# Sample attention of the even mixer: four sequences side by side in four column groups, page transposes placed behind the queries

## The chip, the core and the metric

The kernel runs on one core of one Trainium2 chip. The metric is the device time of one execution in microseconds (us). Engines are named as in the profile: PE (TensorE matmuls), PEld (TensorE weight loads), DVE (VectorE), ACT (ScalarE), POOL (GpSimd), SP (SyncE, which issues most DMAs).

## What is computed

The reference is one inference step of a two-layer decoder trunk for a prompt of 512 tokens and for 8 short sample sequences of 4 tokens each. The 32 sample tokens ride beside the prompt as columns 512 to 543 of every activation. Layer 0 (even) has a stick-breaking attention beside an RG-LRU; layer 1 (odd) a gated DeltaNet. A SwiGLU block stands before and behind each mixer.

The change touches one part: the attention of the sample tokens over their cached past. Each of the 8 sequences has 256 past positions in two pages of 128, found through a page table:

```python
past_k = cache_k[e][page_table].reshape(nb_s, n_pages * PAGE_SIZE, SB_HEADS, SB_HEAD_DIM)
past_v = cache_v[e][page_table].reshape(nb_s, n_pages * PAGE_SIZE, SB_HEADS, SB_HEAD_DIM)
...
z = jnp.einsum('bqhd,bshd->bhqs', q, k, preferred_element_type=jnp.float32) * (SB_HEAD_DIM ** -0.5)
z = z + bias.astype(jnp.float32)[None, :, None, None]
mask = k_pos[None, :] < q_pos[:, None]
log_keep = jnp.where(mask, jax.nn.log_sigmoid(-z), 0.0)
later = lax.cumsum(log_keep, axis=3, reverse=True) - log_keep
w = jnp.where(mask, jnp.exp(jax.nn.log_sigmoid(z) + later), 0.0)
return jnp.einsum('bhqs,bshd->bqhd', w.astype(v.dtype), v)
```

## The kernel before

All large products are three fp32r matmuls each (high and low halves of both operands): `mm3`, lines 362 to 364, output tile `lin`, with 256 or 288 columns a pass. Almost all of the kernel's time is these. The weights come in by `W` (tile `raw`, by SP), are split by ACT (line 323, `wh`) and DVE (line 324, `wl`). The output goes to one of two PSUM buffers in the even mixer, and DVE takes it away (line 646 for queries, keys and values).

The even mixer (`even_mixer`) issues its steps in the order of a string:

```python
EVEN_ORDER = "Q0 L0 V0 A0 Q1 V1 A1 Q2 X0 L1 F L2 G0 G1 G2 L3 X1 X2 G3 X3 E S0 S1 S2 V2 S3 A2 Q3 K0 V3 P2 P3 K1 A3 W U P0 P1 O1 T O0"
```

Q, V, L and X are projections, A0 to A3 the prompt's attention for one pair of heads each (`prompt_attention`: tiles `z` and `pv`, softmax-like chains on ACT and DVE between the matmuls), S the LRU scans on DVE. K0 and K1 are the sample scores of four sequences each, W the weights from them, U the sums over the values. O1 and O0 are the two halves of the output projection: O1 takes the LRU's part, O0 the attention's, whose second column half holds the sample tokens and so needs U's result.

A list scheduler turns this into one fixed order for each engine: it takes instructions by the priority of the string as soon as its own model says that their inputs and buffers are there, and may pull later work forward. Within an engine the instructions then run in that order, and each waits for semaphores that were set when the program was built.

**Scores, `sample_scores` (lines 741 to 763).** For each sequence `b` and each of its two pages: `page` (line 736) issues an indirect DMA of 256 KB by POOL into a tile of 128 positions by 512 (8 heads of 64); four transposes on PE (line 751) put it into PSUM tile `tp`; ACT (line 755) or DVE (line 753) copies it to `kt`. Then four matmuls in plain fp32 (line 758, tile `sc`), one for each pair of heads, accumulate the sequence's 32 rows (8 heads by 4 queries) by 256 positions. The output stands in partitions 32(b mod 4) to 32(b mod 4)+31, so the matmul uses one 32-wide column group of the array. DVE copies each sequence's rows to `zs` (line 759). A plain fp32 matmul is two passes (two records in the profile); the fp32r ones are one.

**Values, `sample_values` (lines 788 to 814).** For each half of four sequences the weights are transposed into `wT`; then for each sequence and page a value page is fetched and one fp32 matmul of 512 columns (line 805, tile `po`) adds into the sequence's 32 partitions. A last matmul (line 806) adds the step's own four tokens, DVE copies `po` to `os` (line 807), and 32 small matmuls (line 812, tile `oT`) turn it round for O0; ACT and DVE split it into `yh` and `yl` (lines 370, 371).

**Page buffers.** Pages share the tag `XP` with the LRU's tiles and with `wT`. There are `PB = 6` of these buffers. A page's DMA waits until the buffer's previous tenant has been read for the last time. PSUM tiles `tp`, `sc`, `sn`, `po` and `oT` share one buffer (tag `s`); `pv` has one of its own.

Of the kernel before, what the change touches and what calls it, by code (L numbers as in the profile page):

```python
# [7 lines left out]
F32 = mybir.dt.float32  # L8
# [3 lines left out]
AF = mybir.ActivationFunctionType  # L12
# [3 lines left out]
P = 128  # L16
# [330 lines left out]
def mm3(E, ws, xh, xl, evac, ks=None, halves=(0, 1)):  # L347

    nc = E.nc
    for h in halves:  # L350
        c0, cn = HALVES[h]
        use = ks[h] if ks is not None else None
        terms = [(w, k) for w in ws for k in w.at if use is None or k in use]
        if use is not None:
            terms.sort(key=lambda t: use.index(t[1]))
        E.nlin += 1
        ps = E.lin[E.nlin % len(E.lin)].tile([P, REST], F32, tag="lin", name=E.nm("lin"))[:, :cn]
        n = ws[0].h.shape[2]
        for i, (w, k) in enumerate(terms):
            wh, wl = w.h[:, w.at[k]], w.l[:, w.at[k]]  # L360
            rh, rl = xh[k][:, c0:c0 + cn], xl[k][:, c0:c0 + cn]
            nc.tensor.matmul(ps[:n], lhsT=wh, rhs=rh, start=(i == 0), stop=False)  # L362
            nc.tensor.matmul(ps[:n], lhsT=wh, rhs=rl, start=False, stop=False)  # L363
            nc.tensor.matmul(ps[:n], lhsT=wl, rhs=rh, start=False, stop=(i == len(terms) - 1))  # L364
        evac(h, c0, cn, ps)


def split_to(E, yh, yl, src, eng="act"):
    nc = E.nc
    nc.scalar.activation(yh, src, AF.Copy)  # L370
    nc.vector.tensor_tensor(yl, src, yh.bitcast(F32), op=ALU.subtract)  # L371
# [11 lines left out]
def ffn_body(E, w_in, w_out, nxt, w0=None, pre=None, mid=None, store=False):  # L383
    nc, tc = E.nc, E.tc
    with tc.tile_pool(name=E.nm("ffn"), bufs=1) as fp:
# [8 lines left out]
        for m in range(16):  # L394
            wg, wu = w0 if m == 0 else (W(E, w_in[:, o:o + P]) for o in (m * P, DFF + m * P))
            sg = fp.tile([P, NT], F32, tag="sg", name=E.nm("sg"), bufs=2)
            pr = fp.tile([P, NT], F32, tag="pr", name=E.nm("pr"), bufs=2)

            def ev_g(h, c0, cn, ps):
                s = sg[:, c0:c0 + cn]  # L400
                nc.vector.tensor_tensor(s, ps, E.rstd[:, c0:c0 + cn], op=ALU.mult)  # L401
                E.act(s, s, AF.Silu)

            def ev_u(h, c0, cn, ps):
                p_ = pr[:, c0:c0 + cn]
                nc.vector.tensor_tensor(p_, ps, E.rstd[:, c0:c0 + cn], op=ALU.mult)  # L406
                nc.vector.tensor_tensor(p_, p_, sg[:, c0:c0 + cn], op=ALU.mult)  # L407
                split_to(E, hh[m][:, c0:c0 + cn], hl[m][:, c0:c0 + cn], p_)

            mm3(E, [wg], E.xh, E.xl, ev_g)  # L410
            mm3(E, [wu], E.xh, E.xl, ev_u)
        if mid is not None:
            mid()
        for m in range(KD):
            ws = []
            for g in range(2):
                w = W(E, w_out[g * D:(g + 1) * D, m * P:(m + 1) * P])
                w.at = {k + 8 * g: i for k, i in w.at.items()}
                ws.append(w)

            def ev(h, c0, cn, ps):
                xx = E.x[m][:, c0:c0 + cn]
                nc.vector.scalar_tensor_tensor(xx, ps, 0.5, xx, op0=ALU.mult, op1=ALU.add)  # L423

            mm3(E, ws, hh, hl, ev)
            if nxt is not None:
                split_x(E, m, *nxt)
            if store:
                store_tile(E, m, *(fp.tile([P, NT], F32, tag=t, name=E.nm("out"), bufs=2) for t in ("sg", "pr")))
# [303 lines left out]
def page(E, ap, name, o):  # L733

    t = ap.tile([P, NE], F32, tag="XP", name=E.nm("page"), bufs=PB)[:, :512]
    E.nc.gpsimd.indirect_dma_start(out=t, out_offset=None, in_=E.I[name].rearrange("a n s h d -> (a n s) (h d)"),
                                   in_offset=bass.IndirectOffsetOnAxis(ap=E.idx[:, o:o + 1], axis=0))
    return t


def sample_scores(E, ap, qb, ks, zs, hf):

    nc = E.nc
    for b in range(4 * hf, 4 * hf + 4):
        rows = slice(32 * (b % 4), 32 * (b % 4) + 32)
        kt = ap.tile([P, 4, 256], F32, tag="kt", name=E.nm("kt"))
        for i in range(2):
            kp = page(E, ap, "cache_k", 2 * b + 1 - i)
            tp = E.pm.tile([P, 4, P], F32, tag="s", name=E.nm("tp"))
            for p in range(4):  # L750
                nc.tensor.transpose(tp[:, p], kp[:, p * P:(p + 1) * P], E.ident)
            if i:
                nc.vector.tensor_copy(kt[:, :, P:], tp)
            else:
                nc.scalar.activation(kt[:, :, :P], tp, AF.Copy)
        ps = E.pm.tile([P, 256], F32, tag="s", name=E.nm("sc"))
        for p in range(4):
            nc.tensor.matmul(ps[rows], lhsT=qb[p][:, b], rhs=kt[:, p], start=(p == 0), stop=(p == 3))  # L758
        nc.vector.tensor_copy(zs[rows, hf, :256], ps[rows])
    ps = E.pm.tile([P, NS], F32, tag="s", name=E.nm("sn"))  # L760
    for p in range(4):
        nc.tensor.matmul(ps, lhsT=qb[p][:, 4 * hf:4 * hf + 4].rearrange("p a b -> p (a b)"), rhs=ks[:, p], start=(p == 0), stop=(p == 3))
    nc.vector.tensor_tensor(zs[:, hf, 256:], ps, E.newmask[:, hf], op=ALU.add)
# [23 lines left out]
def sample_values(E, ap, zs, vs, yh, yl):  # L787
    nc = E.nc
    os = ap.tile([P, 2, 512], F32, tag="kt", name=E.nm("os"))
    for hf in range(2):  # L790
        wps = E.m([P, 2, P])
        for i in range(2):
            nc.tensor.transpose(wps[:, i], zs[:, hf, P * i:P * i + P], E.ident)
        wps2 = E.m([NS, P])
        nc.tensor.transpose(wps2, zs[:, hf, 256:], E.ident)
        wT = ap.tile([P, NE], F32, tag="XP", name=E.nm("wT"), bufs=PB)[:, :3 * P].rearrange("p (a b) -> p a b", a=3)
        nc.vector.tensor_copy(wT[:, :2], wps)
        nc.gpsimd.memset(wT[NS:64, 2], 0.0)
        nc.scalar.activation(wT[:NS, 2], wps2, AF.Copy)
        po = E.pm.tile([P, 512], F32, tag="s", name=E.nm("po"))  # L800
        for g in range(4):
            b = 4 * hf + g
            for i in range(2):
                vp = page(E, ap, "cache_v", 2 * b + 1 - i)
                nc.tensor.matmul(po[32 * g:32 * g + 32], lhsT=wT[:, i, 32 * g:32 * g + 32], rhs=vp, start=(i == 0), stop=False)  # L805
        nc.tensor.matmul(po, lhsT=wT[:64, 2], rhs=vs[:64], start=False, stop=True)
        nc.vector.tensor_copy(os[:, hf], po)
    oT = E.pm.tile([P, 4, NS], F32, tag="s", name=E.nm("oT"))
    for hf in range(2):
        for h in range(8):  # L810
            j = h % 2
            nc.tensor.matmul(oT[64 * j:64 * j + 64, h // 2, 16 * hf:16 * hf + 16], lhsT=os[:, hf, 64 * h:64 * h + 64], rhs=E.sel[:, h], start=True, stop=True)
    for p in range(4):
        split_to(E, yh[p][:, T:], yl[p][:, T:], oT[:, p])
# [8 lines left out]
def even_mixer(E, w_in, w_out, nxt):  # L823
    nc, tc, O = E.nc, E.tc, E.O
    with tc.tile_pool(name=E.nm("evy"), bufs=1) as yp:
# [3 lines left out]
        with E.phase(4, 2), tc.tile_pool(name=E.nm("att"), bufs=1) as ap:  # L829
# [51 lines left out]
            for tok in EVEN_ORDER.split():  # L881
# [7 lines left out]
                elif c == "L":  # L889
                    L[i] = lru_linear(E, ap, w_in, i)  # L890
                elif c == "X":
                    X[i] = lru_gate_in(E, ap, w_in, i)
                elif c == "F":
                    gw = lru_gate_weights(E)
                    E.table("sigmoid_and_others")
                elif c == "G":
                    gate[i] = lru_gates(E, ap, gw, i, *L[i])
                elif c == "E":
                    E.table("gelu_apprx_tanh_and_others")
                    for t in range(4):  # L900
                        E.act(X[t], X[t], AF.Gelu_apprx_tanh)
                    E.table(LNEXP)
                elif c == "S":
                    lru_scan(E, i, *gate[i], X[i])
                elif c == "T":
                    lru_state(E)
                elif c == "P":
                    split_to(E, yh[4 + i], yl[4 + i], X[i])
                elif c == "K":
                    if i == 0:  # L910
                        zs = ap.tile([P, 2, 288], F32, name="zs")
                    sample_scores(E, ap, qb, ks, zs, i)
                elif c == "W":
                    sample_weights(E, ap, zs)
                elif c == "U":
                    sample_values(E, ap, zs, vs, yh, yl)
                elif c == "O":
                    out(i)
# [748 lines left out]
```

## Time and profile before

| | us |
|---|---|
| median of 3 runs | 1933.24 (1932.34 to 1935.51) |
| profiled execution | 1937.59 |
| its span (first to last instruction) | 1935.8 |
| PE busy in the span | 1878.8 (97%) |
| DVE, ACT, POOL busy | 1082.1, 836.9, 125.1 |
| mean granted share of TensorE's clock | 0.989 |

The chain of work that ended last runs through PE for 84% of the span. The places of the change lie at 320 to 326 us and at 383 us (a few page transposes that the scheduler pulled forward), at 483 to 555 us (K0 and K1) and at 563 to 596 us (U). In the timeline a row is the engine's start, length, line, operation, tiles, shape and count, with the idle time before it and what ended that in brackets. A matmul's length holds its whole pipeline; what it costs in a stream is the distance from its start to the start of the next.

### The profile page before, as it was taken

To read this page: it belongs to the slowest core of one execution; us is meant where nothing else is said; L and a number is where in the kernel's file an instruction comes from. 1 tells how busy PE (TensorE), PEld (TensorE's weight loads), DVE (VectorE), ACT (ScalarE), POOL (GpSimd) and SP (SyncE) were. 2 spreads that over 40 slices of the span, in tenths; PEclk is the share of its full clock that TensorE was granted. 3 is DMA by queue.
4 is the path that set the end of the run, shared out by engine and by line. 5 is a ranking of instruction groups with operands and counts; after the bars stand their busy time and mean duration, and the time that the engine had idled before them with its cause. 6 is when DMAs were issued, how large, how long until landed. Compare 5 with 4: busy or idle time off the path is not lost.

```text
span 1935.8 us, 36595 instructions
## 1 busy us (share of the span) xinstructions
PE 1878.8 (97%) x15037; PEld 1799.5 (93%) x15037; DVE 1082.1 (56%) x2563; ACT 836.9 (43%) x1733; POOL 125.1 (6%) x237
## 2 busy tenths in 40 slices
PE   7999999999899999999999999899998997999999
PEld 6999999889668999999999999899998997999998
DVE  7444334786756544433544433688978858444422
ACT  6333324777744433322433322466675646333221
POOL 0000002111320000000000000112111100000000
PEclk9999999999999999999999999899999998999999
DMA  4333233322332333323333322333343322233332
GB/s 131 89 87 90 77 88 94 90 59 73 88 103 84 88 88 88 88 81 89 102 88 88 88 81 78 89 86 94 97 132 78 94 78 66 80 88 88 87 111 67
DMA packets 315972, 171.03 MB, mean 88 GB/s; under 512 B 28470, under 2 KB 310278, under 8 KB 315804
## 3 DMA queue, kind: packets, MB, share of 16 engines
q1 hardware_dynamic: 313244, 160.30, 29.5%
q0 software_dynamic: 2560, 8.39, 1.5%
q8 instruction: 118, 1.93, 0.4%
q14 instruction: 50, 0.41, 0.1%
HBM read 158.01 MB, written 10.65 MB: 87 GB/s over the span
## 4 chain that ended last, share of the span: by engine, by line
PE 84%; DVE 8%; ACT 4%; DMA 2%; issue 2%; POOL 1%; SPq 0%; ACTq 0%; DVEq 0%; POOLq 0%
PE lin L362 25%; PE lin L363 24%; PE lin L364 24%; DVE wl L324 1%; PE pv L729 1%; PE sc L758 1%; PE po L805 1%; DVE LT L1224 1%; DVE acc L1106 1%; DMA raw<-in_w_in_odd 1%; DVE ltmp L1223 1%; ACT wh L323 1%; PE s L1451 1%; DMA raw<-in_w_ffn_in 0%; PE m L1183 0%
## 5 line engine op out<-in xcount | busy, mean ns | idle before, releaser
L362 PE MATMUL lin<-xh,wh 128*128 128x256 f32 (+2 forms) x2992 | 875.1, 293 | 19.1 <-DVE sz L1537 4.5
L363 PE MATMUL lin<-xl,wh 128*128 128x256 f32 (+2 forms) x2992 | 872.8, 292 | 0.6 <-DVE xl L371 0.3
L364 PE MATMUL lin<-xh,wl 128*128 128x256 f32 (+2 forms) x2992 | 867.1, 290 | 0.5 <-DVE wl L324 0.5
L362 PEld LDWEIGHTS lin<-xh,wh 128*128 128x128 f32 (+1 forms) x2992 | 566.8, 190 | 25.9 <-ACT wh L323 9.0
L364 PEld LDWEIGHTS lin<-xh,wl 128*128 128x128 f32 (+1 forms) x2992 | 567.8, 190 | 5.9 <-issue 4.1
L363 PEld LDWEIGHTS lin<-xl,wh 128*128 128x128 f32 (+1 forms) x2992 | 566.9, 189 | 4.5 <-issue 1.7
L323 ACT ACTIVATE wh<-raw 128x1024 fp32r<-128x1024 f32 x261 | 275.8, 1057 | 498.9 <-PE lin L363 419.4
L324 DVE TENSOR_TENSOR wl<-raw,wh 128x1024 fp32r<-128x1024 f32 x261 | 317.7, 1217 | 89.9 <-PE lin L364 88.0
L362 PE MATMUL lin<-hh,wh 128*128 128x288 f32 (+1 forms) x1024 | 295.7, 289 | 0.0
L363 PE MATMUL lin<-hl,wh 128*128 128x288 f32 (+1 forms) x1024 | 295.4, 288 | 0.0
L364 PE MATMUL lin<-hh,wl 128*128 128x288 f32 (+1 forms) x1024 | 294.9, 288 | 0.0
L363 PEld LDWEIGHTS lin<-hl,wh 128*128 128x128 f32 x1024 | 193.0, 188 | 0.2
L364 PEld LDWEIGHTS lin<-hh,wl 128*128 128x128 f32 x1024 | 192.7, 188 | 0.1
L362 PEld LDWEIGHTS lin<-hh,wh 128*128 128x128 f32 x1024 | 192.5, 188 | 0.1
L401 DVE TENSOR_TENSOR sg<-lin,rstd 128x256 f32<-128x256 f32 (+1 forms) x128 | 55.9, 438 | 162.5 <-PE lin L364 162.4
L406 DVE TENSOR_TENSOR pr<-lin,rstd 128x256 f32<-128x256 f32 (+1 forms) x128 | 56.5, 441 | 155.9 <-PE lin L364 155.7
L370 ACT ACTIVATE hh<-pr 128x256 fp32r<-128x256 f32 (+1 forms) x128 | 55.1, 431 | 202.4 <-DVE pr L407 202.1
L423 DVE SCALAR_TENSOR_TENSOR x<-lin,x 128x256 f32<-128x256 f32 x64 | 28.2, 441 | 168.7 <-PE lin L364 168.7
L371 DVE TENSOR_TENSOR hl<-pr,hh 128x256 fp32r<-128x256 f32 (+1 forms) x128 | 56.6, 442 | 61.9 <-ACT hh L370 61.8
L100 ACT ACTIVATE sg<-sg 128x256 f32<-128x256 f32 (+1 forms) x128 | 53.7, 422 | 54.8 <-DVE sg L401 54.8
L267 ACT ACTIVATE xh<-x,vec 128x544 fp32r<-128x544 f32 (+2 forms) x64 | 39.6, 632 | 75.1 <-DVE x L423 59.3
L1106 DVE SCALAR_TENSOR_TENSOR acc<-XP,cw,acc 128x568 f32<-128x568 f32 x72 | 58.8, 817 | 2.1 <-ACT acc L1104 1.8
(480 smaller groups left out, 2098.5 us busy)
## 6 DMA issues: line engine op xcount, KB each, us to landing
raw<-in_w_ffn_in SPq DMA_DIRECT2D x128, 512.0 KB
raw<-in_w_ffn_out SPq DMA_DIRECT2D x64, 512.0 KB
raw<-in_w_in_odd SPq DMA_DIRECT2D x32, 512.0 KB
raw<-in_w_in_even SPq DMA_DIRECT2D x20, 512.0 KB
raw<-in_w_out_even SPq DMA_DIRECT2D x8, 512.0 KB
S<-in_state_dn_S SPq DMA_DIRECT2D x8, 512.0 KB
out_dn_S_sample<-S SPq DMA_DIRECT2D x8, 512.0 KB
raw<-in_w_out_odd SPq DMA_DIRECT2D x8, 512.0 KB
```

The lines of the kernel that those rows point to most:

```text
L100: i = self.nc.scalar.activation(out, in_, func, **kw).ins
L267: nc.scalar.activation(xh, x, AF.Copy, scale=g)
L323: nc.scalar.activation(self.h, raw, AF.Copy)
L324: nc.vector.tensor_tensor(self.l, raw, self.h.bitcast(F32), op=ALU.subtract)
L362: nc.tensor.matmul(ps[:n], lhsT=wh, rhs=rh, start=(i == 0), stop=False)
L363: nc.tensor.matmul(ps[:n], lhsT=wh, rhs=rl, start=False, stop=False)
L364: nc.tensor.matmul(ps[:n], lhsT=wl, rhs=rh, start=False, stop=(i == len(terms) - 1))
L370: nc.scalar.activation(yh, src, AF.Copy)
L371: nc.vector.tensor_tensor(yl, src, yh.bitcast(F32), op=ALU.subtract)
L401: nc.vector.tensor_tensor(s, ps, E.rstd[:, c0:c0 + cn], op=ALU.mult)
L406: nc.vector.tensor_tensor(p_, ps, E.rstd[:, c0:c0 + cn], op=ALU.mult)
L1106: nc.vector.scalar_tensor_tensor(a, XP[:, j:j + XW - 3], cw[j], a, op0=ALU.mult, op1=ALU.add)
```

## The change

Scores: for each half of four sequences and each page position `i`, four pages (one a sequence) are fetched first. For each pair of heads `p`, one PSUM tile `tp` takes one transposed block of each of the four sequences, is copied to `kt`, and four matmuls of 128 columns go to the four column groups of one PSUM tile. That tile, `sc`, now has the tag of the prompt attention's `pv`, and is copied once for all four sequences. The transposes of a tile are chained in the scheduler's order (`E.after` is an ordering edge on one engine with no semaphore), beginning with the page that is fetched last, and in K0 they may not stand ahead of the last projection matmul that was issued, that of Q3. Values: for each page position four pages are fetched, and their four matmuls are chained likewise. Number, shape and columns of the value matmuls stay; the 32 score matmuls of 256 columns become 64 of 128.

```diff
--- before.py
+++ after.py
@@ -361,7 +361,7 @@
             rh, rl = xh[k][:, c0:c0 + cn], xl[k][:, c0:c0 + cn]
             nc.tensor.matmul(ps[:n], lhsT=wh, rhs=rh, start=(i == 0), stop=False)
             nc.tensor.matmul(ps[:n], lhsT=wh, rhs=rl, start=False, stop=False)
-            nc.tensor.matmul(ps[:n], lhsT=wl, rhs=rh, start=False, stop=(i == len(terms) - 1))
+            E.last_mm = nc.tensor.matmul(ps[:n], lhsT=wl, rhs=rh, start=False, stop=(i == len(terms) - 1)).ins
         evac(h, c0, cn, ps)
 
 
@@ -741,22 +741,25 @@
 def sample_scores(E, ap, qb, ks, zs, hf):
 
     nc = E.nc
-    for b in range(4 * hf, 4 * hf + 4):
-        rows = slice(32 * (b % 4), 32 * (b % 4) + 32)
-        kt = ap.tile([P, 4, 256], F32, tag="kt", name=E.nm("kt"))
-        for i in range(2):
-            kp = page(E, ap, "cache_k", 2 * b + 1 - i)
+    sc = E.pm.tile([P, 512], F32, tag="pv", name=E.nm("sc"))[:, :256]
+    for i in range(2):
+        kp = [page(E, ap, "cache_k", 2 * (4 * hf + b) + 1 - i) for b in range(4)]
+        for p in range(4):
+            if p % 2 == 0:
+                kt = ap.tile([P, 2, 4, P], F32, tag="kt", name=E.nm("kt"))
             tp = E.pm.tile([P, 4, P], F32, tag="s", name=E.nm("tp"))
-            for p in range(4):
-                nc.tensor.transpose(tp[:, p], kp[:, p * P:(p + 1) * P], E.ident)
-            if i:
-                nc.vector.tensor_copy(kt[:, :, P:], tp)
+            tr = [nc.tensor.transpose(tp[:, b], kp[b][:, p * P:(p + 1) * P], E.ident).ins for b in (3, 0, 1, 2)]
+            for j in range(1, 4):
+                E.after(tr[j], tr[j - 1])
+            if hf == 0:
+                E.after(tr[0], E.last_mm)
+            if p % 2:
+                nc.vector.tensor_copy(kt[:, 1], tp)
             else:
-                nc.scalar.activation(kt[:, :, :P], tp, AF.Copy)
-        ps = E.pm.tile([P, 256], F32, tag="s", name=E.nm("sc"))
-        for p in range(4):
-            nc.tensor.matmul(ps[rows], lhsT=qb[p][:, b], rhs=kt[:, p], start=(p == 0), stop=(p == 3))
-        nc.vector.tensor_copy(zs[rows, hf, :256], ps[rows])
+                nc.scalar.activation(kt[:, 0], tp, AF.Copy)
+            for b in range(4):
+                nc.tensor.matmul(sc[32 * b:32 * b + 32, i * P:(i + 1) * P], lhsT=qb[p][:, 4 * hf + b], rhs=kt[:, p % 2, b], start=(p == 0), stop=(p == 3), skip_group_check=True)
+    nc.vector.tensor_copy(zs[:, hf, :256], sc)
     ps = E.pm.tile([P, NS], F32, tag="s", name=E.nm("sn"))
     for p in range(4):
         nc.tensor.matmul(ps, lhsT=qb[p][:, 4 * hf:4 * hf + 4].rearrange("p a b -> p (a b)"), rhs=ks[:, p], start=(p == 0), stop=(p == 3))
@@ -798,12 +801,12 @@
         nc.gpsimd.memset(wT[NS:64, 2], 0.0)
         nc.scalar.activation(wT[:NS, 2], wps2, AF.Copy)
         po = E.pm.tile([P, 512], F32, tag="s", name=E.nm("po"))
-        for g in range(4):
-            b = 4 * hf + g
-            for i in range(2):
-                vp = page(E, ap, "cache_v", 2 * b + 1 - i)
-                nc.tensor.matmul(po[32 * g:32 * g + 32], lhsT=wT[:, i, 32 * g:32 * g + 32], rhs=vp, start=(i == 0), stop=False)
-        nc.tensor.matmul(po, lhsT=wT[:64, 2], rhs=vs[:64], start=False, stop=True)
+        for i in range(2):
+            vp = [page(E, ap, "cache_v", 2 * (4 * hf + g) + 1 - i) for g in range(4)]
+            mm = [nc.tensor.matmul(po[32 * g:32 * g + 32], lhsT=wT[:, i, 32 * g:32 * g + 32], rhs=vp[g], start=(i == 0), stop=False, skip_group_check=True).ins for g in (3, 0, 1, 2)]
+            for j in range(1, 4):
+                E.after(mm[j], mm[j - 1])
+        nc.tensor.matmul(po, lhsT=wT[:64, 2], rhs=vs[:64], start=False, stop=True, skip_group_check=True)
         nc.vector.tensor_copy(os[:, hf], po)
     oT = E.pm.tile([P, 4, NS], F32, tag="s", name=E.nm("oT"))
     for hf in range(2):
```

Behind the even mixer the order is the same on every engine. Three places in the built order, whose names are tiles with the build's numbers:

PE in K0, before: a sequence's four score matmuls (`sc`) stand together, and transposes (`tp`) of the next sequence's pages follow at some distance (`m` is another transpose).

```order
L758 MATMUL sc_5810<-kt_5793,qb_4622 32x256
L758 MATMUL sc_5810<-kt_5793,qb_5752 32x256
L364 MATMUL lin_5901<-xh_90,wl_5871 128x288
L362 MATMUL lin_5901<-xh_91,wh_5870 128x288
L363 MATMUL lin_5901<-xl_99,wh_5870 128x288
L364 MATMUL lin_5901<-xh_91,wl_5871 128x288
L362 MATMUL lin_5901<-xh_92,wh_5870 128x288
L363 MATMUL lin_5901<-xl_100,wh_5870 128x288
L364 MATMUL lin_5901<-xh_92,wl_5871 128x288
L751 MATMUL tp_5819<-ident,page_5817 128x128 x4
```

PE in K0, now: here the last set of transposes of the first half (`tp_5861`) and what comes behind it.

```order
L761 MATMUL sc_5770<-kt_5850,qb_4622 32x128 x4
L751 MATMUL tp_5861<-ident,page_5827 128x128
L751 MATMUL tp_5861<-ident,page_5821 128x128
L751 MATMUL tp_5861<-ident,page_5823 128x128
L751 MATMUL tp_5861<-ident,page_5825 128x128
L362 MATMUL lin_6507<-xh_92,wh_6503 128x256
L721 MATMUL z_6115<-sl_6127,negtri 128x384
L725 MATMUL z_6115<-sh_6084,negones 128x128
L726 MATMUL z_6115<-sl_6085,negones 128x128
L725 MATMUL z_6115<-sh_6104,negones 128x256
L761 MATMUL sc_5770<-kt_5850,qb_5752 32x128 x4
L765 MATMUL sn_5872<-ks,qb_3639 128x32
```

The score matmuls stand in 16 sets of four. The next transposes, `tp_5964` on the pages 5961, 5955, 5957 and 5959, come behind 18 more rows (three `sn`, ten `lin`, four `z` and an identity load). What stands between sets is O1's projection (`lin_6507`), which stood in U before.

PE in U, before: around the value matmuls (`po`) of the first half's last sequence.

```order
L805 MATMUL po_6265<-page_6284,wT_6261 32x512
L363 MATMUL lin_6515<-xl_98,wh_6483 128x256
L364 MATMUL lin_6515<-xh_90,wl_6484 128x256
L720 MATMUL z_6165<-sh_6176,negtri 128x256
L362 MATMUL lin_6515<-xh_91,wh_6483 128x256
L363 MATMUL lin_6515<-xl_99,wh_6483 128x256
L364 MATMUL lin_6515<-xh_91,wl_6484 128x256
L721 MATMUL z_6165<-sl_6177,negtri 128x256
L725 MATMUL z_6165<-sh_6156,negones 128x128
L726 MATMUL z_6165<-sl_6157,negones 128x128
L805 MATMUL po_6265<-page_6287,wT_6261 32x512
L806 MATMUL po_6265<-vs,wT_6261 128x512
```

PE in U, now: from the last value matmul of the second chain to the end of U.

```order
L806 MATMUL po_6285<-page_6302,wT_6281 32x512
L809 MATMUL po_6285<-vs,wT_6281 128x512
L806 MATMUL po_6321<-page_6328,wT_6317 32x512
L806 MATMUL po_6321<-page_6322,wT_6317 32x512
L806 MATMUL po_6321<-page_6324,wT_6317 32x512
L806 MATMUL po_6321<-page_6326,wT_6317 32x512
L806 MATMUL po_6321<-page_6340,wT_6317 32x512
L806 MATMUL po_6321<-page_6334,wT_6317 32x512
L806 MATMUL po_6321<-page_6336,wT_6317 32x512
L806 MATMUL po_6321<-page_6338,wT_6317 32x512
L809 MATMUL po_6321<-vs,wT_6317 128x512
L815 MATMUL oT_6348<-sel,os_6275 64x16 x16
```

The projection and the attention matmuls that stood between the value matmuls are gone. Ahead of the first row shown stand the last `pv` of A3, the first chain (pages 6292, 6286, 6288, 6290), three `lin`, four `m`, and the rest of the second chain (pages 6304, 6298, 6300).

POOL in U, now: the order in which the value pages are issued (`wT` rows are a small memset, which needs a buffer of the same six).

```order
L736 DMA page_6288<-in_cache_v,idx 128x512
L736 DMA page_6290<-in_cache_v,idx 128x512
L736 DMA page_6292<-in_cache_v,idx 128x512
L736 DMA page_6298<-in_cache_v,idx 128x512
L736 DMA page_6300<-in_cache_v,idx 128x512
L736 DMA page_6302<-in_cache_v,idx 128x512
L736 DMA page_6304<-in_cache_v,idx 128x512
L801 MEMSET wT_6317 32x128
L736 DMA page_6322<-in_cache_v,idx 128x512
L736 DMA page_6324<-in_cache_v,idx 128x512
L736 DMA page_6326<-in_cache_v,idx 128x512
```

It is the same kind of row as before, one behind the other; what differs is who frees the buffer that each one waits for. By the semaphores of the built program, pages 6288, 6290, 6292 and 6298 take the buffers of the last four key pages; 6300, 6302, 6304 and `wT_6317` those of the first value chain; 6322, 6324, 6326 and 6328 those of the second; and of the last four pages one takes the first `wT`'s and three those of the third chain. In K0 and K1, likewise, the pages 5825 and 5827 wait for the transposes `tp_5811`, 5959 and 5961 for `tp_5861`, 6009 and 6011 for `tp_5995`, each the last set on four pages.

## Rows read from the trace of the kernel before

**Rows 1.** The page, first lines: span and busy time of each engine.

```profile
span 1935.8 us, 36595 instructions
...
PE 1878.8 (97%) x15037; PEld 1799.5 (93%) x15037; DVE 1082.1 (56%) x2563; ACT 836.9 (43%) x1733; POOL 125.1 (6%) x237
```

**Rows 2.** Timeline of PE, scores of one sequence: start us, length us, instruction.

```profile
512.56 1.91 PE L758 MATMUL sc<-kt,qb 128*32 128x256 f32 x8
514.40 0.40 PE L364 MATMUL lin<-xh,wl 128*128 128x288 f32 x1
```

**Rows 3.** Timeline of PE, value matmuls: one, three and two together.

```profile
567.36 1.05 PE L805 MATMUL po<-page,wT 128*32 128x512 f32 x2
568.34 1.13 PE L729 MATMUL pv<-wt,vz 128*128 128x512 f32 x2
...
571.05 1.90 PE L805 MATMUL po<-page,wT 128*32 128x512 f32 x6
572.88 0.41 PE L362 MATMUL lin<-xh,wh 128*128 128x288 f32 x1
...
581.98 1.90 PE L805 MATMUL po<-page,wT 128*32 128x512 f32 x4
583.82 0.44 PE L720 MATMUL z<-sh,negtri 128*128 128x384 f32 x1
```

**Rows 4.** Timeline of PE and DVE, early page transposes.

```profile
324.25 0.82 PE L751 MATMUL tp<-ident,page 128*128 128x128 f32 x4 [1.81 <-DMA page<-in_cache_k,idx]
325.86 0.45 PE L751 MATMUL tp<-ident,page 128*128 128x128 f32 x1 [0.78 <-ACT kt L755]
...
326.53 0.41 PE L364 MATMUL lin<-xh,wl 128*128 128x256 f32 x1
...
323.96 1.22 DVE L324 TENSOR_TENSOR wl<-raw,wh 128x1024 fp32r<-128x1024 f32 x1
```

**Rows 5.** Stretches: us, busy of PE, PEld, DVE, ACT, POOL, granted clock, DMA share, GB/s.

```profile
320.00:340.00 20.00, 16.92 (x108) 15.88 (x108) 11.43 (x22) 11.10 (x24) 6.08 (x11) 0.83 0.33 93
...
480.00:490.00 10.00, 7.24 (x44) 5.87 (x43) 9.11 (x19) 5.93 (x13) 7.18 (x14) 0.92 0.32 86
```

**Rows 6.** Timeline of PE, three early score matmuls and what follows.

```profile
483.00 1.48 PE L758 MATMUL sc<-kt,qb 128*32 128x256 f32 x6
487.18 0.36 PE L362 MATMUL lin<-xh,wh 128*128 128x256 f32 x1 [2.70 <-DVE f L646]
```

**Rows 7.** Timeline of POOL in U, page issues.

```profile
568.68 0.94 POOL L736 DMA_INDIRECT page<-in_cache_v,idx  x1 [16.90 <-PE po L805]
...
583.30 0.94 POOL L736 DMA_INDIRECT page<-in_cache_v,idx  x1 [0.71 <-PE po L805]
584.55 0.95 POOL L736 DMA_INDIRECT page<-in_cache_v,idx  x1 [0.30 <-PE z L720]
```

**Rows 8.** DMA issues, 530 to 600 us: count, median us from issue to landing.

```profile
page<-in_cache_v,idx POOLq DMA_INDIRECT x16, 3.3
```

**Rows 9.** Timeline of PE, projection matmuls of 256 and 288 columns.

```profile
479.59 0.28 PE L364 MATMUL lin<-xh,wl 128*128 128x256 f32 x1
479.71 0.29 PE L362 MATMUL lin<-xh,wh 128*128 128x288 f32 x1
479.84 0.29 PE L363 MATMUL lin<-xl,wh 128*128 128x288 f32 x1
```

**Rows 10.** Chain that ended last: start us, length us, work of four or more matmuls.

```profile
507.28 0.44 PE tp L751 x4
...
528.02 0.83 PE sn L762 x8
...
592.70 1.05 PE po L806 x2
...
595.15 1.04 PE oT L812 x32
```

**Rows 11.** Tiles os and oT: ns min/median/max, first and last start us, forms.

```profile
L807 DVE COPY os<-po x2: 692/692/692, 580.9 to 593.8; 128x512 f32<-128x512 f32 x2
...
L370 ACT ACTIVATE yh<-oT x4: 190/198/198, 596.2 to 598.7; 128x32 fp32r<-128x32 f32 x4
```

**Rows 12.** Waits of PE, 300 to 620 us: total us, times, longest us.

```profile
PE z L720 <- ACT sh L370: 1.9, 4, 0.7
```

## The prediction

> **What bounds the kernel now.** I began with the first lines of the page [rows 1]: PE is busy 97% of the span, every other engine at most 56%. So work taken from PE's stream is time, and so is every new wait in it. PE runs its instructions in a fixed order: if one waits for a page, all behind it wait too. The question is what each piece costs in the stream, and what stands behind it.
>
> The timeline gives prices, always from start to start. One sequence's scores, eight passes of 256 columns, take 512.56 to 514.40, 1.84 us [rows 2]. One value matmul, two passes of 512 columns, takes 0.98; two matmuls of one sequence take 1.84 [rows 3]. So a pass of 512 columns costs (1.84 - 0.98) / 2 = 0.43, and going to a column group and back 0.12. By columns a pass of 256 costs 0.215 (8 x 0.215 + 0.12 = 1.84, as seen) and one of 128 0.11. The third piece of rows 3 is the important one: six passes, four in one sequence's group and two in the next one's, take 1.83, no more than four. Two column groups ran fully side by side.
>
> POOL's timeline gives the price of a page. Issues that wait for nothing else start 1.25 us apart (583.30, 584.55), and data lands 3.3 us behind the issue [rows 7, 8]. The first issue starts about 0.34 behind the matmul that frees its buffer (568.34 to 568.68) [rows 3, 7].
>
> **Term 1, early transposes.** In the old order PE stood 1.81 us for a page and 0.78 for a copy at 322 to 326 us [rows 4]. But the next projection needs its low weights, which DVE finishes at 323.96 + 1.22 = 325.18; its third matmul ran at 326.53. Without the transposes it can run at 325.2: **-1.3**. The clock was at 0.83 of full in that stretch [rows 5], which is 2 x 0.17 x 20 = 6.8 us at 1.2 GHz, 2.6 of them idle; the other 4.2 cost 2.1 more. PE still waits there, about as long, so I don't count that, and keep -3.4 as the other end. The eight transposes that stood early (five here, three at 383 us, which filled a wait for DVE) now stand in K0: 8 x 0.11 [rows 10], **+0.9**.
>
> **Term 2, scores.** Before, 8 x 1.84 = 14.7. Now 16 sets of four. If four groups run side by side, a set costs two passes of 128 and the switch, 2 x 0.11 + 0.12 = 0.34, in all 5.4: a gain of 9.3. The three score matmuls at 483.00 (1.4 us) gave nothing to gain: behind them PE waited 2.70 for DVE, and that wait only grows [rows 6]. **-7.9**. If nothing overlapped, 128 passes would cost 14.1 and the switches 1.9, a loss.
>
> **Term 3, page waits in K0 and K1.** Four pages are read by four sets of transposes and all come free at the last one. With six buffers two of the next four can be there already; the other two are issued only then. They need 0.34 + 1.25 + 3.3 = 4.9 us. In the order I counted what PE has meanwhile, at 0.12 and 0.13 a projection matmul [rows 9], 0.34 a score set and 0.83 the four `sn` [rows 10]: about 3.1, 3.4 and 3.0 us at the three places. Waits of 1.8, 1.5 and 1.9: **+5.2** (0 if other stalls of PE cover them; 7 if POOL is late).
>
> **Term 4, the attention's chains.** ACT and DVE have the same prompt attention to do in less PE time. PE waited for its softmax four times, 1.9 us in all [rows 12]; `sc` now also waits for A2's `pv` to be read, and A3's `pv` for K1's scores. I nearly double it: **+1.5** (0 to 4).
>
> **Term 5, value matmuls.** Before, eleven pieces like those of rows 3: eight of 0.98, one of 1.84, two of 1.83: 13.3 us. Now four chains of 2 x 0.43 and three switches: 3.8. **-9.5**.
>
> **Term 6, page waits in U.** This decides. Each chain reads its four pages at once, so their buffers come free at once, and the next pages are only then issued, 1.25 us apart. Chain 2 needs three that wait for chain 1: 0.34 + 2 x 1.25 + 3.3 = 6.1 us; PE has three `lin` and four `m` for that, 0.8, and stands 5.3. Chain 3 needs four: 7.4, less the 1.05 of the new tokens' matmul [rows 10]: 6.35. Chain 4 needs three: 6.1, with nothing between. **+17.8**. Before, the same fetches lay behind projections and A3, which now stand in K0 and K1 or ahead of U. What is left, O0, waits for A3 and for this very result.
>
> **Term 7, the end of U.** `os` (0.69), `yh` and `yl` of the first heads (0.2 each) [rows 11] and four handovers lay beside O1's matmuls; now O0 waits for them: **+1.6**. The 1.04 of `oT` [rows 10] was on PE before too.
>
> **Term 8, the clock.** Waits of 1.81 and 0.78 us left PE at the lower level for 6.8 us; behind one of 2.70 the stretch shows 0.92 of 10 us [rows 4, 5, 6]. I expect three waits of 5 to 6 us, with a microsecond of work between, to hold 1.2 GHz till the end of U: three chains of 0.86, the last 1.05 and `oT`'s 1.04 take twice, 4.7, and some projections behind. **+5** (0 if the clock stays up; 8 with 7 us of projections at half).
>
> **The sum.** -1.3 + 0.9 - 7.9 + 5.2 + 1.5 - 9.5 + 17.8 + 1.6 + 5 = **+13.3 us**. On the profiled execution that is 1937.59 + 13.3 = 1950.9; the median of the runs lies 4.35 lower, so the forecast is 1933.24 + 13.3 = **1946.5**.
>
> **Rivals.** A measurement of this kernel can tell about 0.2%, 3.9 us, from no change.
>
> *Passes in strict order.* If a sequence's second pass held back the next sequence's first, four matmuls would take five steps, not two: a score set +0.33, a value chain +1.29, together 16 x 0.33 + 4 x 1.29 = 10.5, and 1957. Against it: by this, the six passes of rows 3 would have taken five steps, 2.27 with the switch; they took 1.83. The Trainium skill has this rule: its page "TensorE: Matmul & The Clock Gate", Part 3 (packing small matmuls), says that matmuls are "strict FIFO, no reordering", in start and end. By that rule the time would be 1957; the row speaks against it for two groups, and no row has four. Chance 0.08.
>
> *Only two at a time.* The trace shows two groups side by side, never four. Then a set costs 0.22 and a chain 0.86 more: +6.9, and 1953. The change would do half of what it says. Chance 0.12.
>
> *Milder waits.* The clock stays up, and K's page waits fall together with waits for ACT: -5 - 5.2, so +3.1 and 1936. For it: in the old U there were no waits at all, so the clock there is a guess. Chance 0.18, a third of it above 1937.1.
>
> *Faster: the pages come in time.* Without the page waits and their clock, -17.8 - 5.2 - 5, the change gives -14.7 and 1918.5. It decides from the point where these three together cost under 14.7, about half of what I count: the wait from a chain's end to the next chain's start would have to be 3 us, less than one landing. For it: all pages but three or four of a chain could be early. Against it: buffers, not bandwidth, hold them back, and the built order leaves nothing to stand between. Chance 0.10.
>
> **Chances.** The forecast has 0.52. Slower by over 0.2%: 0.52 + 0.08 + 0.12 + 0.06, with a little taken off, 0.77. Within 0.2%: the rest of the mild case, 0.12. Faster: 0.11. The range, 1936 to 1954, takes in the mild case and two groups at a time, the bounds of the clock and of term 4, and leaves out strict order and the faster case, under 2 in 10.
>
> **What would show it.** Right: in U, three gaps of PE before `po` of 5 to 6.5 us that end on page DMAs, at a lower granted clock; in K, gaps of about 2 us before transposes that end on page DMAs; a score set of 0.34 from start to start. Wrong: `po` chains with no gap before them, a set that takes 0.55 or more, or a clock of 1.00 through U.

## The result and the profile after

The changed kernel takes 1948.19 us (median of 4 runs, 1946.91 to 1949.05) against 1932.82: ratio 1.0076, 95% interval 1.0059 to 1.0094. A second set of runs gave 1949.62 us and 1.0079 (1.0062 to 1.0095). It is slower by 15 us, inside the forecast's range (1946.5; 1936 to 1954).

The page of the changed kernel, first lines, to be read against [rows 1]:

```profile
span 1945.1 us, 36707 instructions
...
PE 1865.0 (96%) x15101; PEld 1794.5 (92%) x15101; DVE 1081.4 (56%) x2557; ACT 837.0 (43%) x1733; POOL 123.2 (6%) x237
```

PE is busy 13.8 us less and the span is 9.3 us longer: what was cut came back as standing time, and more. Whole spans scatter, though (a second profile of the kernel before has 1938.4, of the changed one 1952.0; in both the clock was low for longer far behind the change, between 1419 and 1446 us). So the comparisons below use **the mixer's time**: from one ACT instruction at 322 us (line 323) to one in the next SwiGLU (line 370, tile `hh`), the same two in every kernel. Each value comes from one profile. In the timeline of ACT, before:

```profile
322.35 1.06 ACT L323 ACTIVATE wh<-raw 128x1024 fp32r<-128x1024 f32 x1 [0.18 <-PE lin L363]
...
704.02 0.45 ACT L370 ACTIVATE hh<-pr 128x288 fp32r<-128x288 f32 x1 [1.01 <-DVE pr L407]
```

and after:

```profile
321.88 1.06 ACT L323 ACTIVATE wh<-raw 128x1024 fp32r<-128x1024 f32 x1 [0.18 <-PE lin L363]
...
714.85 0.45 ACT L370 ACTIVATE hh<-pr 128x288 fp32r<-128x288 f32 x1 [1.01 <-DVE pr L407]
```

That is 381.7 and 393.0, +11.3; the second profiles give 380.6 and 393.4, +12.8. One kernel's two values lie within 1.1 us of each other, so differences of that size say nothing.

The timeline of PE in U (start us, length us, instruction, idle before and its releaser):

```profile
580.50 1.06 PE L806 MATMUL po<-page,wT 128*32 128x512 f32 x8
581.50 0.38 PE L362 MATMUL lin<-yh,wh 128*128 128x256 f32 x1
...
588.38 1.94 PE L806 MATMUL po<-page,wT 128*32 128x512 f32 x8 [5.45 <-DMA page<-in_cache_v,idx]
590.24 2.07 PE L809 MATMUL po<-vs,wT 64*128 64x512 f32 x2
...
597.89 1.94 PE L806 MATMUL po<-page,wT 128*32 128x512 f32 x8 [5.57 <-DMA page<-in_cache_v,idx]
...
606.12 1.93 PE L806 MATMUL po<-page,wT 128*32 128x512 f32 x8 [6.29 <-DMA page<-in_cache_v,idx]
607.98 2.07 PE L809 MATMUL po<-vs,wT 64*128 64x512 f32 x2
610.84 1.89 PE L815 MATMUL oT<-sel,os 128*64 128x16 f32 x32 [0.78 <-DVE os L810]
613.03 0.82 PE L362 MATMUL lin<-yh,wh 128*128 128x288 f32 x2 [0.30 <-ACT yh L370]
```

The first chain runs 580.50 to 581.50: eight passes of 512 columns in four groups take 1.00 us, where one sequence's two passes took 0.98 [rows 3]. All four groups run side by side. If a sequence's second pass held back the next sequence's first, the chain would take five steps, 2.27 (estimated from [rows 3]); this row speaks against that. The Trainium skill says that matmuls start and end in strict order ("TensorE: Matmul & The Clock Gate", Part 3). The trace's starts agree pass by pass: the four first passes start one behind the other at 580.50 to 580.52, the four second ones at 580.96 to 580.98. What does not hold is the reading behind the rival *strict order*, that both passes of one matmul come ahead of the next matmul. The later chains take 1.86, at half clock (1.2 GHz). Ahead of each stands a wait for a page.

POOL's timeline shows why those pages are late:

```profile
581.82 0.95 POOL L736 DMA_INDIRECT page<-in_cache_v,idx  x1 [12.23 <-PE po L806]
583.08 0.95 POOL L736 DMA_INDIRECT page<-in_cache_v,idx  x1 [0.31 <-PE m L635]
...
590.57 0.95 POOL L736 DMA_INDIRECT page<-in_cache_v,idx  x1 [5.07 <-PE po L806]
...
600.05 0.94 POOL L736 DMA_INDIRECT page<-in_cache_v,idx  x1 [3.53 <-PE po L806]
```

POOL stands idle for 12, 5 and 3.5 us until a chain ends, then issues one page each 1.25 us. PE and POOL wait for each other in turn. The stretches (columns as in [rows 5]) show the clock. Before, in the second half of U:

```profile
590.00:600.00 10.00, 10.00 (x76) 6.65 (x75) 4.39 (x10) 3.33 (x8) 0.00 (x0) 1.00 0.17 54
```

and after:

```profile
570.00:580.00 10.00, 9.51 (x61) 7.79 (x59) 7.82 (x16) 5.84 (x10) 0.00 (x0) 1.00 0.17 60
580.00:590.00 10.00, 4.45 (x25) 1.18 (x23) 2.04 (x4) 0.86 (x2) 3.06 (x4) 0.85 0.40 124
590.00:600.00 10.00, 4.25 (x14) 0.73 (x10) 0.69 (x1) 0.00 (x0) 4.73 (x5) 0.50 0.46 131
600.00:610.00 10.00, 3.88 (x10) 0.70 (x10) 0.00 (x0) 0.00 (x0) 2.84 (x3) 0.50 0.28 79
610.00:620.00 10.00, 8.92 (x71) 8.76 (x71) 3.04 (x9) 2.24 (x7) 0.00 (x0) 0.62 0.01 2
```

PE's waits from 300 to 640 us by releaser, the view of [rows 12] (total us, times, longest):

```profile
PE po L806 <- DMA page<-in_cache_v,idx: 17.3, 3, 6.3
...
PE tp L751 <- DMA page<-in_cache_k,idx: 3.8, 3, 1.9
```

And K, where a score set takes 530.06 to 530.41, 0.35 us:

```profile
530.06 0.43 PE L761 MATMUL sc<-kt,qb 128*32 128x128 f32 x8
530.41 0.66 PE L751 MATMUL tp<-ident,page 128*128 128x128 f32 x4
...
536.34 0.63 PE L751 MATMUL tp<-ident,page 128*128 128x128 f32 x4 [1.93 <-DMA page<-in_cache_k,idx]
```

### The profile page after: what moved, and what is told of

Its sections match the earlier page's. It is cut to its first block, busy times and chain, and to the rows that moved or that the text cites. A ratio compares the mean times of both kernels' runs of the same rounds, so it can differ in the third digit from the quotient of the medians.

```text
span 1945.1 us, 36707 instructions
## 1 busy us (share of the span) xinstructions
PE 1865.0 (96%) x15101; PEld 1794.5 (92%) x15101; DVE 1081.4 (56%) x2557; ACT 837.0 (43%) x1733; POOL 123.2 (6%) x237
## 4 chain that ended last, share of the span: by engine, by line
PE 57%; DVE 5%; issue 1%; ACT 1%; DMA 1%; POOL 0%; SPq 0%; ACTq 0%; DVEq 0%; POOLq 0%
PE lin L362 18%; PE lin L363 17%; PE lin L364 17%; DVE wl L324 1%; DVE LT L1227 1%; DMA raw<-in_w_in_odd 1%; DVE acc L1109 1%; DVE ltmp L1226 1%; PE s L1454 1%; PE m L1186 0%; PE c L1324 0%; DMA grs<-gdr 0%; ACT wh L323 0%; DVE Dt L1141 0%; DVE Dn L1140 0%
## 5 line engine op out<-in xcount | busy, mean ns | idle before, releaser
L267 ACT ACTIVATE xh<-x,vec 128x544 fp32r<-128x544 f32 (+2 forms) x64 | 39.6, 632 | 75.1 <-DVE x L423 59.3
```

The lines of the kernel that those rows point to most:

```text
L267: nc.scalar.activation(xh, x, AF.Copy, scale=g)
```

## The experiments

The theory: four buffers that come free together, with nothing left on PE to stand between, cost more than the chains save. Rivals: the loss sits in K; the clock falls in U whatever the waits; the chains themselves are dear. The diffs below are cut to their main lines, with `...` for what is left out.

**1. Value products one by one, scores as changed.** One hunk of the change is undone:

```diff
-            vp = [page(E, ap, "cache_v", 2 * (4 * hf + g) + 1 - i) for g in range(4)]
...
+        for g in range(4):
...
+                vp = page(E, ap, "cache_v", 2 * b + 1 - i)
+                nc.tensor.matmul(po[32 * g:32 * g + 32], lhsT=wT[:, i, 32 * g:32 * g + 32], rhs=vp, start=(i == 0), stop=False)
```

> The changed kernel with the value products one matmul after another, a group at a time, as before the change; the scores stay in four groups. Theory: each page buffer comes free as its own matmul ends, so pages are asked for one by one at POOL's 1.25 us each and land beside the matmuls; PE's idle time before po falls from 17.3 to 6 to 10 us, the matmuls cost 13.3 us at full clock where the chains cost 3.8, and the time comes to 1946 (1938 to 1950): the chains' gain of 9.5 was worth no more than what their releases in fours cost. Rival 1 (the loss sits in K): as much as the chains gained is lost now, 1957. Rival 3 (the four-group chains are what costs): 1934 or less.

Measured: 1935.63 us, ratio 1.0012 (1.0002 to 1.0022); mixer 379.8. That is below the expected range, and within 2 us of what the third rival had: the waits fell further than expected. Waits, and the stretch that had been at 0.50:

```profile
PE tp L751 <- DMA page<-in_cache_k,idx: 3.6, 3, 2.0
...
PE po L808 <- DMA page<-in_cache_v,idx: 1.4, 4, 0.4
...
590.00:600.00 10.00, 7.81 (x23) 1.37 (x23) 0.69 (x1) 0.00 (x0) 3.20 (x4) 1.00 0.47 131
```

The same pages through the same six buffers, behind the same K: the waits in U go from 17.3 to 1.4 and the clock stays up. With the scores as changed, the value chains bring the loss; the rivals that seat it in K, or give U a low clock of its own, fall. That the chains are dear in themselves is not ruled out by this run, but by the first chain's 1.00 us and by experiment 2.

**2. More buffers for value pages.** Six of the 16 stay late; the expectation's four is a miscount of mine.

```diff
+VTAGS = (("XP", "XP", "XP", "XP"), ("f", "f", "qk", "qk"), ("XP", "XP", "XP", "f"), ("f", "f", "qk", "qk"))
...
+    if tag == "f":
+        t = E.f()[:, :512]
...
```

> The changed kernel with its value pages in three kinds of buffers (the six page buffers, four of the feature buffers, two of the buffers for queries and keys), so that all but four of the 16 value pages are asked for ahead of U and none of those waits for a chain to release its buffer. Nothing else is changed. Theory (released in fours, asked for one after another, no work beside): the three waits of 5.45, 5.57 and 6.29 us before the chains of po fall to under 1 us each, the clock from 580 to 610 us of the span stays above 0.9, and the time falls by the 17.3 us of waits and 3 to 7 us of clock, to 1925 (1922 to 1932). Rival 1 (the loss sits in K and the attention pairs): 1944 or more, with the waits gone. Rival 2 (the clock falls in U whatever the waits are): waits gone, granted clock in 580 to 610 still under 0.85, 1931 or so. A miss of the edit itself: the value pages now stand ahead of four key pages in POOL's order; if those come late, K's page waits rise from 3.8 us by up to 10 and eat the gain.

Measured: 1932.53 us, 0.9991 (0.9982 to 1.0001); mixer 380.5. The time is just above the expected range: the waits fell, but not all to under 1 us, and the clock did not stay above 0.9. U's waits fall by 14.0, K's rise by 1.4:

```profile
PE tp L754 <- DMA page<-in_cache_k,idx: 5.2, 3, 2.1
PE po L809 <- DMA page<-in_cache_v,idx: 3.3, 3, 2.5
...
590.00:600.00 10.00, 6.47 (x34) 1.87 (x34) 0.69 (x1) 0.00 (x0) 1.38 (x2) 0.70 0.26 77
```

The cause is confirmed by a second way, without touching the chains. With one wait of 2.5 us left, the stretch reads 0.70.

**3. Projection kept back for U.**

```diff
+            if i == 0 and behind is not None:
+                E.after(first, behind)
```

> The changed kernel with the first matmul of O1's output projection, from its fifth group on, held behind K1's last score matmul, so that some 12 us of projection are left to stand between U's chains; buffers and pages as in the changed kernel. Theory (no work left beside the page waits): projection fills two of the three waits, PE's idle time before po falls from 17.3 us to 5 to 8, the granted clock there stays near 1, and the time falls by 10 to 15 us to 1936 (1932 to 1940). The work held back must be missed somewhere: if it was cover for K's page waits, K's idle time rises by up to 4 us. Rival 1 (the loss sits in K and the attention pairs): 1946 or more, whatever U's waits do. Rival 3 (chains over four groups cost more than rows read): waits fall but each chain stays above 1.5 us at full clock, 1940 or more.

Measured: 1953.13 us, 1.0102 (1.0085 to 1.0119); mixer 396.3. A miss, and of the wrong sign: the mixer is 3 us slower than the changed kernel's. The waits in U do halve:

```profile
PE po L809 <- DMA page<-in_cache_v,idx: 8.7, 2, 5.0
...
520.00:560.00 40.00, 32.02 (x261) 23.97 (x259) 18.82 (x36) 20.19 (x40) 10.81 (x12) 0.90 0.36 112
590.00:600.00 10.00, 8.69 (x31) 5.52 (x32) 1.57 (x3) 0.00 (x0) 4.74 (x5) 0.50 0.41 125
```

But K loses the same projection: PE is busy 32.0 us of 520 to 560 instead of 36.0, its clock falls there, and in U the work kept back runs at half speed behind a wait that it does not fill. Here the work beside a wait was not spare; moving it moved the wait.

**4. Value chains alone.** Only the second hunk of the change in `sample_values`, K as before.

> The kernel before with the value chains of the change alone; scores, transposes and the early ordering stay as before. In its order projection and attention matmuls stand between U's chains. Theory: the releases in fours are there too, but with work beside them; the chains give back some of their 9.5 us, idle time before po stays under 8 us in all, 1929 (1924 to 1937). If the chains were a loss of their own (rival 3, or waits that no cover fills), 1940 or more. Rival 1 (loss in K): 1923, the whole gain.

Measured: 1931.4 us, 0.9990 (0.9980 to 1.0000); mixer 379.9. This lies in the expected range. With the old K, waits before `po` are 4.4 us in all: the chains neither lose nor win beyond the scatter.

**5. Early ordering alone**, and **the kernel before again**.

```diff
+                if hf == 0:
+                    E.after(tr, E.last_mm)
```

> The kernel before with one thing of the change: K0's page transposes stand behind the last projection matmul. Scores and values as before. By the prediction's Term 1 the gain is 1.3 us at most: 1932 (1930 to 1934). By the profile of the changed kernel, which stands some 4 us ahead of the kernel before from 340 us on and keeps 3.5 to 4 of it at 480 us, it is 3 to 4.5 us: 1929 (1928 to 1930.5). If the work that no longer covers K's score waits costs as much as the early stretch gains, 1933 or more, with the idle time found in 475 to 560 us.

> The kernel before itself, for a second profile of it: its first profiled execution was 1937.6 us against a median of 1932.8. If those 4.8 us are one execution's own clock, the new profile's granted clock in 300 to 340 us is above the 0.91 of the first and its span is 1930 to 1933; if they belong to every profiled execution, the span is near 1935.8 again. Either way the time is 1933.

Measured for the early ordering: 1932.15 us, 0.9990 (0.9976 to 1.0003), no clear change; mixer 378.6, that is 2.0 and 3.1 less than the two profiles of before. Before again: 1936.22 us, 1.0003 (0.9987 to 1.0019); span 1938.4, which fits neither of the two spans expected, with the clock at 1.00 in 300 to 340 us and 0.97 in 340 to 400, where the first profile had 0.91 and 1.00. The same waits for key pages stand in it:

```profile
323.38 0.66 PE L751 MATMUL tp<-ident,page 128*128 128x128 f32 x4 [1.61 <-DMA page<-in_cache_k,idx]
```

and 0.92 behind them, but the clock fell only at 381.7 us. The early dip is not fixed to a place, and the 4 us by which the changed kernel seemed ahead at 340 us were in part the first profile's own clock.

**6. Value chains and early ordering, old scores; the same with more buffers; and the buffers without the chains.**

> The kernel before with the value chains and the early ordering of the change, but its scores one sequence after another. In its order attention and projection matmuls stand in front of each of U's chains, without holding anything back by hand. Theory (release in fours costs only what nothing covers): the four buffers still come free together, but idle time before po stays under 4 us, the clock in U near 1, and the gains of both parts show: 1926 (1922 to 1929). Rival 3 (value chains a loss of their own): no better than the early ordering alone, 1929 or more. If the early ordering moves U's cover forward (as it does K's), waits of 8 us or more in U and 1934 or more.

> As the kernel with the value chains and the early ordering, with ten of the 16 value pages in buffers that are free ahead of U. Theory: waits before po under 2 us, 1925 (1921 to 1928), the same as without the buffers within 2 us where work already covers the waits. Its order leaves less work between the chains of U, so if six pages are still late the waits are 3 to 6 us and the clock in U falls as in the changed kernel with more buffers (0.70 in 590 to 600): 1929 or more.

> A control: early ordering and ten value pages in other buffers, but scores and value products both one after another as in the kernel before. There were no waits on value pages with these products (0.2 us in all with the early ordering alone), so by the theory early pages alone are worth nothing: 1932 (1930 to 1934), as the early ordering alone; the 7 us of the kernel with value chains, early ordering and buffers come from the chains. If the buffers help by themselves (pages that land in a quieter stretch, POOL freed): 1928 or less.

Measured: 1936.36 (1.0012, 0.9998 to 1.0026; mixer 380.1), 1926.70 (0.9957, 0.9944 to 0.9971; 372.3) and 1927.69 us (0.9964, 0.9950 to 0.9977; 373.7). The first is a miss: work stands between the chains, yet PE waits 7.1 us for value pages, 4.2 of it before the second chain:

```profile
PE po L805 <- DMA page<-in_cache_v,idx: 7.1, 3, 4.2
```

So releases in fours cost 7.1 us of waits under the old scores and 17.3 under the new ones, which take the work from between the chains. The second came as expected. The last is a miss too, and the most telling one: with no chain at all, early pages gain about as much as with it (the two intervals overlap). The timeline of PE in U, first with the early ordering alone, where a matmul stands by itself (0.97 from start to start):

```profile
573.49 1.05 PE L807 MATMUL po<-page,wT 128*32 128x512 f32 x2
574.46 0.39 PE L363 MATMUL lin<-xl,wh 128*128 128x256 f32 x1
```

then with early pages, still one by one in the code:

```profile
573.15 0.62 PE L810 MATMUL po<-page,wT 128*32 128x512 f32 x1
573.16 0.62 PE L810 MATMUL po<-f,wT 128*32 128x512 f32 x1
...
575.01 1.12 PE L811 MATMUL po<-vs,wT 64*128 64x512 f32 x2
```

Between 573.15 and 575.01 lie six matmuls, 12 passes: 0.31 us each instead of 0.97. With pages there early the scheduler put them next to each other, and neighbours in different column groups then run side by side without a chain.

**7. The whole change, with key pages in more buffers too.** The tags of the value pages are set anew as well.

```diff
+KTAGS = (("XP", "XP", "XP", "XP"), ("XP", "XP", "qk", "qk"), ("f", "f", "f", "f"), ("XP", "XP", "XP", "XP"))
```

> The whole change (scores and values in four groups, early ordering) with key pages as well as value pages in other buffers: K's third step of four in feature buffers, half of its second in those for queries and keys, so that 12 of 16 key pages are asked for before K's second step starts, and 11 value pages ahead of U. Theory: K's page waits fall from 3.8 us to under 1.5, U's from 17.3 to under 4, the mixer gets the scores' 7.9 us back: 1922 (1917 to 1928). If every microsecond cut from PE in K and U only lays open another wait (attention's ACT and DVE chains, the last pages, the clock at 0.5 to 0.8), 1928 to 1934, no better than the kernel with the old scores.

Measured: 1929.64 us (1921.76 to 1938.38), 0.9969 (0.9949 to 0.9988); mixer 375.6. That misses the expected 1922 (1917 to 1928) and lies in the alternative. PE's waits:

```profile
PE po L809 <- DMA page<-in_cache_v,idx: 2.0, 1, 2.0
PE sc L764 <- DVE kt L760: 2.0, 2, 1.8
PE z L721 <- DVE sl L371: 1.7, 1, 1.7
```

No wait on a key page is left (ten value pages were early, not 11), but DVE is late instead, in K, as the second half of the expectation had it. The clock was at 0.50 from 588.4 to 598.7 us. The changed kernel itself was run once more beside it:

> The changed kernel itself, on the same chip as these two, for a narrower interval and a second profile: 1947 to 1949; its waits before po again 17 us in all, and the clock in 590 to 610 again 0.5.

Measured: 1949.62 us; waits before `po` 17.1, clock 0.50 from 590 to 610.

**Side by side.** Mixer's time in us, all with the early ordering:

| | values one by one | value chains | chains, early pages |
|---|---|---|---|
| old scores | 378.6 | 380.1 | 372.3 |
| scores in four groups | 379.8 | 393.0, 393.4 | 380.5 |

Old scores, one by one and early pages: 373.7. So the scores cost 1.2 alone and the chains 1.5 alone, each about the scatter; both together cost 14.4 to 14.8. And where the time goes from about 508 to 510 us (where ACT makes `ka`, line 690) to the end of the second `xh` of the next SwiGLU (line 267): from each PE matmul's start to the next one's, summed by tile, so that a wait counts with the matmul ahead of it:

| | `sc` | `po` | `lin` | `tp` | others | sum |
|---|---|---|---|---|---|---|
| early ordering alone | 12.9 | 15.0 | 40.6 | 4.6 | 25.8 | 98.9 |
| + scores | 5.6 | 19.0 | 44.5 | 5.3 | 25.5 | 99.8 |
| + scores, chains (the change) | 5.6 | 23.5 | 47.4 | 5.3 | 31.7 | 113.4 |
| + buffers, one by one | 12.9 | 9.9 | 39.6 | 4.6 | 26.1 | 93.1 |
| + buffers, chains | 12.9 | 8.2 | 40.7 | 4.6 | 26.2 | 92.6 |

The scores save their 7.3 us, and `lin` (3.6 us of waits for key pages behind it) and `po` (2.9 us of waits between and behind its matmuls, and fewer neighbours) take 7.9 back.

## Why the prediction was right

For Term 1, PE after, at the place where the early transposes stood:

```profile
323.29 0.38 PE L362 MATMUL lin<-xh,wh 128*128 128x256 f32 x1 [1.31 <-DVE f L646]
```

- **Term 1** (-1.3, and +0.9 in K0) was too small: the early ordering gained 2.0 to 3.1 us of the mixer (one profile; the medians show no clear change). The bound was misread. The low weights that DVE finishes at 325.18 are not those that the next projection needs: after, that projection waits for DVE's `f`, and its third matmul ran at 323.63, when DVE had just begun the same row (323.51, 1.22 us long). From the `wh` row where the mixer's time starts to the projection's first matmul it takes 1.41 us, against 3.61 before (325.96) and 3.33 in its second profile: 1.9 to 2.2 us, not 1.3. Some of the mixer's gain is clock: it spends 10.2 us at 1.2 GHz in each profile of before, 3.4 with the early ordering.
- **Term 2** (-7.9): 12.9 to 5.6 us of `sc`, -7.3; a set takes 0.35, predicted 0.34.
- **Term 3** (+5.2): 3.8, and 3.3 in the second profile. Right in kind, the waits are shorter.
- **Term 5** (-9.5): the first chain's 1.00 says 4.0 us for four at full clock, -9.3. Right as a sum for this change.
- **Term 6** (+17.8): 17.3 and 17.1; 5.45, 5.57, 6.29 against 5.3, 6.35, 6.1. This term decided, and experiments 1 and 2 showed its cause by two ways.
- **Term 7** (+1.6): 0.78 and 0.30, together 1.1.
- **Term 8** (+5): three chains 0.86 each, the last `vs` matmul 1.0, `oT` 0.85 (1.89 for 1.04 [rows 10]), and projections at half clock until about 617 us, 2.2: near 6.7. That the clock falls in U was right; the ground given for it was weak, for the same early waits left the clock at 1.00 in the second profile of before (experiment 5).
- **Term 4** (+1.5) is not seen apart: PE's waits of `z` and `pv` for ACT are 1.9 us in all, as before; the second profile has one more wait of 1.6, of `tp` for DVE. Experiment 7 shows that K's chains on DVE do come next.

The mixer became 11.3 to 12.8 us slower, predicted 13.3. The other terms as measured add up to 8.5 to 10.3; Term 4 and what else there is must make up the rest. Terms 1 and 3 erred one way and Terms 2 and 8 the other, so that the sum comes this near is in part luck. The medians differ by 15.4 and 16.2. No run places the 3 to 4 us more: behind the mixer, where the order is the same, the two profiles of before took 1231.8 and 1236.1 us and those of the changed kernel 1230.3 and 1237.2, and the interval of the ratio reaches down to 11.4 us.

The rival *strict order* fell with the first chain's 1.00, and *two at a time* with it. *Milder waits* fell with the clock at 0.50. *Pages in time*, 1918.5, was not tested in full: with 12 of the 16 key pages and ten value pages asked for early the whole change came to 1929.64, with 2.0 us of waits for a value page, DVE late and the clock at 0.50 for 10 us. But the gain that it counts looks too large. It takes Term 5 as a gain that stands when the waits go, and Term 5's 9.5 is the price of matmuls that stood alone. With early pages and the old scores the one-by-one order costs 9.9 for all `po` against 8.2 with chains, so there the chains are worth 1.7 us of PE.

## What to carry to other kernels

Running products side by side made their inputs' buffers come free together; with six buffers a steady flow of loads became a burst, and PE and the issuing queue waited for each other in turn. Before merging, count from a step's end to the next step's last landing, and the work that the fixed order leaves there; that work is shared, so two savings that each break even can lose together. Try the buffers first: here loads that were early let neighbours overlap without rewriting the products. The two best kernels keep the old scores and take the early ordering and ten early value pages, with value chains (1926.70 us, 0.9957) or without (1927.69 us, 0.9964): about 0.4% below before, and not told apart.

## What the runs showed of the hardware

Four column groups of plain fp32 matmuls run side by side, also where the code issues the matmuls one by one: six adjacent matmuls of 32 by 512 took 1.86 us, a chain of four 1.00, one alone 0.97. To stand together is not always enough: four neighbours with the early ordering alone took 2.31 us (581.19 to 583.51). And a wait can cost twice: behind 3.66 us of standing (experiment 3) the projections kept back for U ran at half clock, with PE busy 8.69 of 10 us. Not every wait does: behind 2.59 us in the first kernel of experiment 6 (until 598.64) the clock was at 1.00, behind 2.02 us in experiment 4 (until 585.09) at 0.50.
